# Layer 1's blocks of gated rows: their sums made in the up projection and loaded by the down projection

## The chip, the core and the metric

The kernel runs on one core of one Trainium2 chip. A core has four compute engines with a queue of instructions each: TensorE (PE, matrix products into PSUM), VectorE (DVE), ScalarE (ACT) and GpSimd (POOL). SyncE (SP) only issues transfers between the chip's memory (DRAM) and SBUF. The metric is the device time of one execution in microseconds, of which the median of several runs is taken. Profiled times of instructions are counted from the first instruction of the program.

## The reference, cut to what matters

Two layers of a diffusion backbone over 1024 tokens of width 1024. Each layer has a mixer (attention) and then a gated MLP with a width-3 convolution. The change is in the MLP of the last layer (layer 1), which has no context rows:

```python
def conv_ffn(x, w_up, conv_w, conv_b, w_down):
    h = x @ w_up                                   # 1024 x 1024 @ 1024 x 5632
    h = lax.conv_general_dilated(h, ...) + conv_b  # along the tokens, width 3
    a, g = jnp.split(h, 2, axis=-1)
    return (jax.nn.silu(g) * a) @ w_down           # 1024 x 2816 @ 2816 x 1024
```

All is float32. Each operand of a product is split into a rounded high part and the rest (`hi`, `lo`), and a product of two such operands takes three matmuls.

## The kernel before, in words

**Both products of the MLP go by a seven-product scheme** (Strassen's, in Winograd's form): each operand is cut in a 2 by 2 grid of blocks, seven products are made of blocks or sums of blocks in the place of eight, and their results are added up. The sums of blocks of `w_down` are made ahead of the layer and stored (`tD`); those of `w_up` are made by POOL when a tile is prepared (`sums`, tile `sw`). Those of the gated rows, which this change is about, are made in the down projection.

**The up projection** (`ffn_up`) goes over 22 tiles j (`NH = 22`), each 128 columns of `a` with the 128 columns of `g` that gate them. `one(j)` makes two of the seven products, `two(j)` the other five. Each product is 12 matmuls of 128x512 (L500 to L502). DVE adds them up in `z` (L479, L572), ACT and DVE make the convolution (L517; L518 and L519, two of each in a tile), ACT the SiLU (L578), DVE the product `silu(g) * a` (L579), and the tile (128 rows of the hidden matrix by 1024 tokens) is stored in DRAM as `hidD[j]` (L580). For layer 1 the first six tiles have their `one` ahead of all `two`s (`pre` is 6), then `one(j)`, `two(j)` follow each other. In this kernel the tiles come in the order 0, 1, 2, ... 21.

**The down projection** (`ffn_down`) sees the hidden matrix as blocks `a11` (tokens 0 to 511, tiles 0 to 10), `a21` (tokens 512 to 1023, the same tiles), `a12` and `a22` (tiles 11 to 21). The contraction goes in three chunks of 3, 4 and 4 tiles k (`CUT`), and in each chunk through the seven products in the order 1, 2, 5, 6, 7, 3, 4; such a pair of chunk and product is called an item here. An item is made for four pairs of token tiles p, so it has 4 times 3 n matmuls with n tiles in the chunk (L875 to L877, into `by` or `bj`). While the products of one item run, `prep` makes the operands of the next: `summed` forms the sum of blocks, in place (on POOL, L686):

```python
5: ("a21", "t1", ("a21", "a22", 1)),   6: ("a21", "t2", ("a21", "a11", 0)),
7: ("a11", "t3", ("a22", "a21", 0)),   3: ("a12", "b22", ("a12", "a21", 0)),
```

(the block that is overwritten, the weight block, and the two terms with 1 for plus), then `hidden` splits it in hi and lo: the rounding on ACT (L121), the rest on DVE (L122, a subtraction of two tiles in SBUF). `weight` does the same for the weight block (tiles `xm`, split into `whi` or `wlo`). In the trace the blocks `a11`, `a12` are called `xb` and `a21`, `a22` are called `a`. `collect` adds the product up in `y` (DVE or POOL, L738; the first copies on ACT, L785); in the last chunk ACT makes the squares for the norm (L337), and `finish` norms, adds the residual (L833) and stores the rows. Blocks are loaded from `hidD` by SP (L668), weight blocks from `w_down` or `tD` (L653).

**What sets the order**: every engine and SP work their queues in order. The order in the queues is made ahead of time by a planner, which follows the program's order and its own estimate of when each instruction could run, so that an instruction without a wait may stand earlier than the program has it. Tiles of a pool with one buffer (`bufs` 1) can be overwritten only when what read them is done. The tiles of the down projection's pool `dn` lie where the up projection's pool `up` was.

Of the kernel before, what the change touches and what calls it, by code (L numbers as in the profile page):

```python
# [12 lines left out]
ALU = mybir.AluOpType  # L13
# [4 lines left out]
P = 128  # L18
T = 1024
# [8 lines left out]
NH = DFF // P  # L28
HF = 512
# [26 lines left out]
class Net:  # L56
# [415 lines left out]

        return [first, lambda: sums(1), lambda: sums(2), lambda: part(load(NH + j) if ctx else load(NH + j)[:, HF:])]

    def ffn_up(self, l, ctx, pre, zb, pool, side=None):

        nc = self.nc
        V, G = nc.vector, nc.gpsimd
        add = lambda o, x, y, e=V: e.tensor_tensor(o, x, y, op=ALU.add)  # L479
        order = [(0, 0), (0, 3)] if ctx else [(0, 0)]  # L480
        order += [(j, 0) for j in range(1, pre)]
        order += [(j, i) for j in range(NH) for i in range(4) if (j, i) not in order]
        steps = [self.up_weights(l, j, ctx, pool, 2 <= j < pre) for j in range(NH)]
        ready, state = {}, {}
        X, Xc = {}, []

        def ahead(n):
            while order and len(ready) < n:
                j, i = order.pop(0)
                ready[j, i] = steps[j][i]()  # L490

        def take(j, i):
            ahead(4)
            return ready.pop((j, i))

        def product(W, v):
            hi, lo = X[v]
            o = self.t(self.by, [P, HF], "by")
            for k in range(4):
                nc.tensor.matmul(o, W[0][:, k, :], hi[k], start=(k == 0), stop=False)  # L500
                nc.tensor.matmul(o, W[0][:, k, :], lo[k], start=False, stop=False)  # L501
                nc.tensor.matmul(o, W[1][:, k, :], hi[k], start=False, stop=(k == 3))  # L502
            return o

        def plain(Ws):
            o = self.t(self.by, [P, HF], "by")[:, :C]
            for k in range(KD):
                W, (hi, lo) = Ws[k // 4], Xc[k]
                nc.tensor.matmul(o, W[0][:, k % 4, :], hi, start=(k == 0), stop=False)  # L509
                nc.tensor.matmul(o, W[0][:, k % 4, :], lo, start=False, stop=False)  # L510
                nc.tensor.matmul(o, W[1][:, k % 4, :], hi, start=False, stop=(k == KD - 1))  # L511
            return o

        def conv(o, z, nt):
            n = z.shape[1]
            cw = lambda i: self.cw[:, l, i, nt:nt + 1]
            nc.scalar.activation(o, z, AF.Identity, scale=cw(1), bias=cw(3))  # L517
            V.scalar_tensor_tensor(o[:, 1:], z[:, :n - 1], cw(0), o[:, 1:], op0=ALU.mult, op1=ALU.add)  # L518
            V.scalar_tensor_tensor(o[:, :n - 1], z[:, 1:], cw(2), o[:, :n - 1], op0=ALU.mult, op1=ALU.add)  # L519

        zt = lambda: self.t(pool(), [P, 1024], "z", zb)
        ot = lambda: self.t(pool(), [P, S if ctx else T], "o", 2)

        def one(j):

            a = take(j, 0)
            p1 = product(a[0], "B11")
            za = zt()
            nc.scalar.copy(za[:, HF:], p1)  # L529
            p2 = product(a[1], "B21")  # L530
            add(za[:, :HF], p2, za[:, HF:])
            oa = og = d = None
            rest = lambda: None
            if ctx:
                def rest():
                    conv(oa[:, T:], plain(a), j)
                if j == 0 or j >= pre:
                    oa = ot()
                    rest()
                if j == 0:  # L540
                    d = take(j, 3)
                    og = ot()
                    conv(og[:, T:], plain(d), NH + j)
            state[j] = za, oa, og, a, d

        def two(j, hook=None):
            za, oa, og, a, d = state.pop(j)
            C11, C12 = za[:, :HF], za[:, HF:]
            S1, S2 = take(j, 1)
            p6 = product(S2, "T2")  # L550
            add(C12, p6, C12)
            S3, S4 = take(j, 2)
            p7 = product(S3, "T3")
            if hook:
                hook()
            zg = zt()
            C21, C22 = zg[:, :HF], zg[:, HF:]
            add(C21, p7, C12)

            p5 = product(S1, "T1")  # L560
            add(C12, p5, C12)
            add(C22, p5, C21)
            p3 = product(S4, "B22")
            add(C12, p3, C12)
            if oa is None:
                oa = ot()
                if ctx:
                    conv(oa[:, T:], plain(a), j)
            conv(oa[:, :T], za, j)
            d = d or take(j, 3)  # L570
            p4 = product(d[0] if not ctx else d[1], "T4")
            V.tensor_tensor(C21, C21, p4, op=ALU.subtract)  # L572
            if og is None:
                og = ot()
                if ctx:
                    conv(og[:, T:], plain(d), NH + j)
            conv(og[:, :T], zg, NH + j)
            nc.scalar.activation(og, og, AF.Silu)  # L578
            self.last_gate = V.tensor_tensor(oa, oa, og, op=ALU.mult)  # L579
            (nc.scalar if j == NH - 1 and not ctx else nc.sync).dma_start(self.hidD[j], oa[:, :T])  # L580
            if ctx:
                c = max(i for i, x in enumerate(self.CUT[:-1]) if x <= j % (NH // 2))
                nc.sync.dma_start(self.hidC[c][j // (NH // 2)][:, :, j % (NH // 2) - self.CUT[c], :], oa[:, T:].rearrange("p (x n) -> p x n", x=2))

        def run(X_, Xc_, hook1, hook2):
            X.update(X_)
            Xc.extend(Xc_ or [])
            for j in range(pre):
                one(j)
            for j in range(NH):  # L590
                if j >= pre:
                    one(j)
                if side:
                    self.steps(side, 1 if j % 4 else 2)
                if j == NH - 1:
                    hook1()
                two(j, hook2 if j == NH - 1 else None)

        return lambda: ahead(2), run

# [28 lines left out]
            self.tc.keep_in_program_order(nc.sync.dma_start(self.tD[l][k], r))  # L629
            yield  # L630

    def ffn_down(self, l, ctx, A, blocks, units):


        nc = self.nc
# [3 lines left out]
        chunks = [range(x, y) for x, y in zip(self.CUT, self.CUT[1:])]  # L639
        res = {}  # L640
        cnt = [0, 0, 0]

        def load_b(c, nm, pin):
            f = int(nm[1]) - 1
# [13 lines left out]
        def weights(n):  # L658

            if n < len(items):  # L660
                load_b(items[n][0], self.FORM[items[n][1]][1], 4 <= n < 7)

        def load_a(c, nm):
            r, h = int(nm[1]) - 1, int(nm[2]) - 1
            res[nm] = []
            for i, k in enumerate(chunks[c]):
                x = blocks(nm, i)
                nc.sync.dma_start(x, self.hidD[k + h * (NH // 2)][:, r * HF:(r + 1) * HF])  # L668
                res[nm].append(x)
            if ctx:  # L670
                n = len(chunks[c])
                x = blocks(nm, 4)[:, :n * P]
                nc.sync.dma_start(x.rearrange("p (k n) -> p k n", k=n), self.hidC[c][h][:, r])
                res[nm].append(x)

        def prep(c, nm):

            a, b, asum = self.FORM[nm]
            n = len(chunks[c])
            nu = n + (1 if ctx else 0)  # L680
            o = ops[c, nm] = [None] * nu, [None] * n

            def summed(name, s, i, e):
                if s:
                    x, y, plus = s
                    e.tensor_tensor(res[name][i], res[x][i], res[y][i], op=ALU.add if plus else ALU.subtract)  # L686

# [49 lines left out]
        def run(src, dst, sink):  # L737
# [101 lines left out]
            for n, (c, nm) in enumerate(items):  # L839
# [4 lines left out]
                for p in range(np_):  # L844
                    if p == 4:
                        for f in early + late:
                            f()
                        early = late = []
                    cnt[2] += 1
                    o = self.t(*((self.by, [P, HF], "by") if cnt[2] % 6 < 4 else (self.bj, [P, HF], "bj")))  # L850
                    multiply(o, c, nm, p, 0, len(chunks[c]))
                    collect(c, nm, p, o)
# [26 lines left out]
    def mlp(self, xa, opA, l, ctx, yT, w_out, src, mid, dst, ahead=None, after=None):  # L879


        nc, tc = self.nc, self.tc
# [2 lines left out]
        A = lambda: self.t(xa, [P, HF], "xm", 16, F32R)  # L885
        mod = self.mod_cols(l, 1)
        halves = lambda x: x.rearrange("p (x n) -> p x n", x=2)
        with ExitStack() as e0:
            pool = lambda name, e: e.enter_context(tc.tile_pool(name=f"{name}{l}", reuse_waits="tile", bufs=1))
            xb = pool("xb", e0)  # L890

# [6 lines left out]
            with self.banks(out=4, turn=2):  # L898
              with self.banks(junk=1, tmp=1):
                with ExitStack() as e1:  # L900
                  xb2 = pool("xd", e1)
                  E = lambda dt=F32: self.t(xb2, [P, HF], "xd", 16, dt)
                  with ExitStack() as e2:
# [28 lines left out]
                      if l == 0:  # L932
                          side = self.ada_queue(lambda: up[0], [(1, b) for b in range(3)], bufs=1, small=lambda tag, p, n: self.t(up[0], [P, 2048], "awr", 1)[:p, :n] if tag == "adar" else self.t(up[0], [p, n], tag, 1),
                                                acc=lambda: self.t(self.bj, [P, HF], "bj"), turn=lambda: self.t(self.bt, [P, 512], "b1"))
                      start, run = self.ffn_up(l, ctx, 2 if ctx else 6, 3 if ctx else 7, lambda: up[0], side)

                      def rows(n):
                          res = []
# [42 lines left out]
                      where = list(range(28, 32)) + list(range(8)) + list(range(12, 16))  # L981
                  blocks = lambda nm, i: B(at[nm] + i).bitcast(F32) if nm in at else self.t(self.pp, [P, HF], f"{nm}_{i}", 1)
                  units = Units(lambda i: B(where[i]), len(where) // 2)
                  load_w, load_h, down = self.ffn_down(l, ctx, A, blocks, units)
                  with ExitStack() as e3:
                      up.append(pool("up", e3))

# [920 lines left out]
```

## Time and profile before

| | us |
|---|---|
| median of 3 runs (lowest, highest) | 2901.68 (2897.69, 2901.73) |
| the profiled execution | 2902.14 |
| its span, first to last instruction | 2900.3 |
| up projection of layer 1 in the trace | about 2243 to 2668 |
| down projection of layer 1 | about 2668 to 2901; last matmul ends at 2885 |

How to read the lines shown below: times are microseconds from the start of the span, means of single instructions are ns. "x11" is a count. `out<-in` are the tiles that an instruction writes and reads, by the program's names without numbers. In square brackets or behind a bar stands the idle time of the engine just ahead of the instruction, with what ended it. PEclk is the share of its clock that TensorE was granted. A row of stretches gives the busy time of each engine within it, so 20 of 20 is an engine without idle time. The ends of matmuls are modelled, and their busy times overlap.

### The profile page before, as it was taken

To read this page: it belongs to the slowest core of one execution; us is meant where nothing else is said; L and a number is where in the kernel's file an instruction comes from. 1 tells how busy PE (TensorE), PEld (TensorE's weight loads), DVE (VectorE), ACT (ScalarE), POOL (GpSimd) and SP (SyncE) were. 2 spreads that over 40 slices of the span, in tenths; PEclk is the share of its full clock that TensorE was granted. 3 is DMA by queue.
4 is the path that set the end of the run, shared out by engine and by line. 5 is a ranking of instruction groups with operands and counts; after the bars stand their busy time and mean duration, and the time that the engine had idled before them with its cause. 6 is when DMAs were issued, how large, how long until landed. Compare 5 with 4: busy or idle time off the path is not lost.

```text
span 2900.3 us, 42828 instructions
## 1 busy us (share of the span) xinstructions
PE 2795.5 (96%) x15699; PEld 2252.0 (78%) x15699; DVE 2125.2 (73%) x2645; ACT 1330.5 (46%) x2373; POOL 1497.5 (52%) x1396
## 2 busy tenths in 40 slices
PE   8999999999999999999989999999998999999997
PEld 6878977776888888878768986666677878887775
DVE  4451255569776777798988768888856898888999
ACT  4321066575333333444457545555556444444443
POOL 2231277446222222165767768888864543332766
PEclk9999999999999999999999999999999999999998
DMA  8366773554223333464244562232253222224642
GB/s 314 127 209 211 242 270 133 197 188 151 79 96 124 118 102 109 167 204 129 75 138 155 148 180 93 101 102 99 84 204 138 73 95 88 88 80 168 202 142 87
DMA packets 235650, 413.89 MB, mean 143 GB/s; under 512 B 28320, under 2 KB 133792, under 8 KB 227504
## 3 DMA queue, kind: packets, MB, share of 16 engines
q1 hardware_dynamic: 212736, 395.61, 40.5%
q10 hardware_dynamic: 22704, 15.55, 1.8%
q8 instruction: 124, 2.03, 0.3%
q14 instruction: 86, 0.70, 0.1%
HBM read 306.16 MB, written 104.92 MB: 142 GB/s over the span
## 4 chain that ended last, share of the span: by engine, by line
PE 55%; DVE 11%; POOL 6%; issue 4%; ACT 2%; DMA 2%; SPq 0%; DVEq 0%; POOLq 0%; ACTq 0%
PE by L500 8%; PE by L501 8%; PE by L502 8%; PE b L1703 4%; PE by L1715 4%; PE b L1684 3%; PE by L877 2%; PE by L875 2%; PE by L876 2%; DVE xb L122 2%; DVE wlo L122 2%; PE by L509 1%; PE by L511 1%; PE by L510 1%; POOL rstd L139 1%
## 5 line engine op out<-in xcount | busy, mean ns | idle before, releaser
L1727 POOL TENSOR_TENSOR part<-part,pT 128x512 f32<-128x512 f32 x192 | 271.6, 1415 | 14.4 <-ACT pT L1704 1.0
L463 POOL TENSOR_TENSOR sw<-wraw,wraw 128x512 f32<-128x512 f32 x44 | 61.0, 1386 | 422.2 <-DVE wlo L122 422.2
L122 DVE TENSOR_TENSOR wlo<-wraw,whi 128x1024 fp32r<-128x1024 f32 (+1 forms) x162 | 221.1, 1371 | 77.4 <-ACT whi L121 77.3
L479 DVE TENSOR_TENSOR z<-by,z 128x512 f32<-128x512 f32 x264 | 176.7, 684 | 106.5 <-PE by L502 103.7
L1704 ACT ACTIVATE pT<-b 128x512 f32<-128x512 f32 x320 | 170.4, 604 | 151.2 <-PE b L1703 137.4
L1685 DVE TENSOR_REDUCE ng<-b 128x1 f32<-128x1280 f32 x122 | 181.7, 1490 | 75.7 <-PE b L1684 75.3
L121 ACT CAST whi<-wraw 128x1024 fp32r<-128x1024 f32 (+1 forms) x162 | 159.5, 990 | 160.8 <-PE b L310 107.0
L500 PE MATMUL by<-xb,whi 128*128 128x512 f32 x528 | 208.0, 394 | 1.7 <-ACT xb L121 1.7
L502 PE MATMUL by<-xb,wlo 128*128 128x512 f32 x528 | 205.9, 390 | 1.0 <-DVE wlo L122 1.0
L501 PE MATMUL by<-xb,whi 128*128 128x512 f32 x528 | 206.2, 391 | 0.3 <-DVE xb L122 0.3
L121 ACT CAST xb<-xb 128x512 fp32r<-128x512 f32 (+2 forms) x184 | 103.2, 567 | 195.2 <-PE by L876 61.6
L615 POOL TENSOR_TENSOR ts<-ts 128x512 f32<-128x512 f32 x88 | 118.3, 1352 | 134.9 <-DMA ts<-in_w_down_dram 133.2
L121 ACT CAST whi<-sw 128x1024 fp32r<-128x1024 f32 x88 | 92.5, 1052 | 202.6 <-PE by L501 173.6
L518 DVE SCALAR_TENSOR_TENSOR o<-z,cw,o 128x1023 f32<-128x1023 f32 x88 | 141.2, 1605 | 48.7 <-ACT o L517 48.6
L122 DVE TENSOR_TENSOR xb<-xb,xb 128x512 fp32r<-128x512 f32 (+2 forms) x184 | 158.9, 879 | 19.4 <-ACT xb L121 18.2
L517 ACT ACTIVATE o<-z,cw 128x1024 f32<-128x1024 f32 x88 | 109.6, 1245 | 130.5 <-DVE z L479 109.0
L460 POOL TENSOR_TENSOR sw<-wraw 128x512 f32<-128x512 f32 x44 | 80.6, 1832 | 167.6 <-DVE wlo L122 124.7
L738 POOL TENSOR_TENSOR y<-y,wraw 128x512 f32<-128x512 f32 x72 | 116.2, 1636 | 94.0 <-DVE wraw L738 59.3
L1715 PE MATMUL by<-pT,Vs 128*64 128x256 f32 x1280 | 150.7, 382 | 0.0
L500 PE MATMUL by<-xm,whi 128*128 128x512 f32 x352 | 138.5, 393 | 4.6 <-ACT z L529 3.2
L500 PE MATMUL by<-xd,whi 128*128 128x512 f32 x352 | 137.4, 390 | 0.4 <-DVE z L479 0.3
L501 PE MATMUL by<-xm,whi 128*128 128x512 f32 x352 | 137.5, 391 | 0.0
(314 smaller groups left out, 8922.0 us busy)
## 6 DMA issues: line engine op xcount, KB each, us to landing
wraw<-in_w_up_t_dram SPq DMA_DIRECT2D x92, 512.0 KB
awr<-in_w_ada_dram SPq DMA_DIRECT2D x44, 1024.0 KB
ts<-in_w_down_dram SPq DMA_DIRECT2D x44, 512.0 KB
tD<-ts SPq DMA_DIRECT2D x22, 1024.0 KB
xm<-tD SPq DMA_DIRECT2D x88, 256.0 KB
hid<-o SPq DMA_DIRECT2D x43, 512.0 KB
xm<-in_w_down_dram SPq DMA_DIRECT2D x66, 256.0 KB
xb<-hid SPq DMA_DIRECT2D x66, 256.0 KB
```

Of the source, the lines that this page charges most:

```text
L121: x = nc.scalar.copy(hi, src) if hi_eng == "s" else nc.vector.tensor_copy(hi, src)
L122: y = (nc.gpsimd if lo_eng == "p" else nc.vector).tensor_tensor(lo, src, hi.bitcast(F32), op=ALU.subtract)
L479: add = lambda o, x, y, e=V: e.tensor_tensor(o, x, y, op=ALU.add)
L500: nc.tensor.matmul(o, W[0][:, k, :], hi[k], start=(k == 0), stop=False)
L501: nc.tensor.matmul(o, W[0][:, k, :], lo[k], start=False, stop=False)
L502: nc.tensor.matmul(o, W[1][:, k, :], hi[k], start=False, stop=(k == 3))
L518: V.scalar_tensor_tensor(o[:, 1:], z[:, :n - 1], cw(0), o[:, 1:], op0=ALU.mult, op1=ALU.add)
L615: sub = lambda o, x, y: nc.gpsimd.tensor_tensor(o, x, y, op=ALU.subtract)
L1685: nc.vector.tensor_reduce(b["ng"][:, h:h + 1], ps[:, :S], axis=AX.X, op=ALU.max, negate=True)
L1704: nc.scalar.activation(b["pT"][:, k], ps, AF.Exp)
L1715: nc.tensor.matmul(out(b["po"][:, :256], i), self.KV[b["g"]][2][:, k], two(b["pT"][:, k], i), start=(k == 0), stop=(k == NT - 1))
L1727: nc.gpsimd.tensor_tensor(x, x if k > 1 else b["pT"][:, 0], b["pT"][:, k], op=ALU.add)
```

## The change

For layer 1 alone, POOL makes the four sums of blocks during the up projection. A generator `hidden_sums` works pair by pair (tile k with tile k + 11): it loads the two tiles of 512 KB from `hidD`, makes the four sums in place in a buffer `hs` (one buffer), and stores the pair of 1 MB in a new DRAM tensor `sD`. So that pairs are complete early, the up projection takes its tiles in the order 0, 11, 1, 12, ... 10, 21. The generator takes its three steps per pair from the fourth tile on: one step after each tile, one more ahead of the `two` of each tile with an even number; what is left (the last two pairs) is done in the first items of the down projection, one step in every second product. In the down projection, `load_a` loads the sum for product 5 from `sD` in the place of `a21`, and `summed` is a load from `sD` of the next sum (256 KB, into the same tile that POOL overwrote before). Layer 0 is left as it was.

```diff
-    def ffn_up(self, l, ctx, pre, zb, pool, side=None):
+    def hidden_sums(self, l, pool):
         nc = self.nc
+        e = lambda o, x, y, op=ALU.subtract: nc.gpsimd.tensor_tensor(o, x, y, op=op)
+        for k in range(NH // 2):
+            r = self.t(pool, [P, 2, T], "hs", 1)
+            for h in range(2):
+                nc.sync.dma_start(r[:, h], self.hidD[k + h * (NH // 2)])
+            yield
+            (x, y), (u, v) = ((r[:, h, :HF], r[:, h, HF:]) for h in range(2))
+            e(v, v, y, ALU.add)
+            e(y, x, y)
+            yield
+            e(x, v, x)
+            e(u, u, x)
+            nc.sync.dma_start(self.sD[l][k], r)
+            yield
+
+    SUM = {5: (1, 1), 7: (0, 1), 6: (0, 0), 3: (1, 0)}
+
+    def ffn_up(self, l, ctx, pre, zb, pool, side=None, hs=None):
+        nc = self.nc
+        seq = [k + h * (NH // 2) for k in range(NH // 2) for h in range(2)] if hs else list(range(NH))
...
-        order += [(j, 0) for j in range(1, pre)]
-        order += [(j, i) for j in range(NH) for i in range(4) if (j, i) not in order]
-        steps = [self.up_weights(l, j, ctx, pool, 2 <= j < pre) for j in range(NH)]
+        order += [(j, 0) for j in seq[1:pre]]
+        order += [(j, i) for j in seq for i in range(4) if (j, i) not in order]
+        steps = {j: self.up_weights(l, j, ctx, pool, 2 <= n < pre) for n, j in enumerate(seq)}
...
-            for j in range(pre):
+            for j in seq[:pre]:
                 one(j)
-            for j in range(NH):
-                if j >= pre:
+            for n, j in enumerate(seq):
+                if n >= pre:
                     one(j)
...
-                two(j, hook2 if j == NH - 1 else None)
+                late = hs and n > 2
+                if late and n % 2 == 0:
+                    next(hs)
+                two(j, hook2 if n == NH - 1 else None)
+                if late:
+                    next(hs)
...
+        def made(x, k, nm):
+            h, r = self.SUM[nm]
+            nc.sync.dma_start(x, sD[k][:, h, r * HF:(r + 1) * HF])
+
         def load_a(c, nm):
...
-                nc.sync.dma_start(x, self.hidD[k + h * (NH // 2)][:, r * HF:(r + 1) * HF])
+                if sD and nm == "a21":
+                    made(x, k, 5)
+                else:
+                    nc.sync.dma_start(x, self.hidD[k + h * (NH // 2)][:, r * HF:(r + 1) * HF])
...
             def summed(name, s, i, e):
-                if s:
+                if s and sD and i < n:
+                    if nm != 5:
+                        made(res[name][i], chunks[c][i], nm)
+                elif s:
                     x, y, plus = s
                     e.tensor_tensor(res[name][i], res[x][i], res[y][i], op=ALU.add if plus else ALU.subtract)
...
                     cnt[2] += 1
+                    if hs and cnt[2] % 2:
+                        next(hs, None)
...
+        self.sD = {}
         with ExitStack() as e0:
+            hsum = None
+            if not ctx:
+                self.sD[l] = [self.t(self.dr, [P, 2, T], f"sD{l}_{k}") for k in range(NH // 2)]
+                hsum = self.hidden_sums(l, e0.enter_context(tc.tile_pool(name=f"hs{l}", reuse_waits="tile", bufs=1, side="right")))
```

More of the change, by code (lines that the diff above doesn't have):

```diff
@@ L536, in rest @@
                     conv(oa[:, T:], plain(a), j)
-                if j == 0 or j >= pre:
+                if j == 0 or j not in seq[:pre]:
                     oa = ot()
@@ L587, in run @@
             Xc.extend(Xc_ or [])
-            for j in range(pre):
+            for j in seq[:pre]:
                 one(j)
-            for j in range(NH):
-                if j >= pre:
+            for n, j in enumerate(seq):
+                if n >= pre:
                     one(j)
                 if side:
-                    self.steps(side, 1 if j % 4 else 2)
-                if j == NH - 1:
+                    self.steps(side, 1 if n % 4 else 2)
+                if n == NH - 1:
                     hook1()
-                two(j, hook2 if j == NH - 1 else None)
+                late = hs and n > 2
[4 more added lines that the diff above has]
+                    next(hs)
         return lambda: ahead(2), run
@@ L630, in down_sums, with ffn_down @@
             yield
-    def ffn_down(self, l, ctx, A, blocks, units):
+    def ffn_down(self, l, ctx, A, blocks, units, hs=None):
         nc = self.nc
@@ L641, in ffn_down @@
         cnt = [0, 0, 0]
+        sD = self.sD.get(l)
         def load_b(c, nm, pin):
@@ L934, in mlp @@
                                                 acc=lambda: self.t(self.bj, [P, HF], "bj"), turn=lambda: self.t(self.bt, [P, 512], "b1"))
-                      start, run = self.ffn_up(l, ctx, 2 if ctx else 6, 3 if ctx else 7, lambda: up[0], side)
+                      start, run = self.ffn_up(l, ctx, 2 if ctx else 6, 3 if ctx else 7, lambda: up[0], side, hsum)
                       def rows(n):
@@ L983, in mlp @@
                   units = Units(lambda i: B(where[i]), len(where) // 2)
-                  load_w, load_h, down = self.ffn_down(l, ctx, A, blocks, units)
+                  load_w, load_h, down = self.ffn_down(l, ctx, A, blocks, units, hsum)
                   with ExitStack() as e3:
```

## The prediction

> **What bounds the kernel now.** The page's first part first: which engine fills the span.
>
> ```profile
> PE 2795.5 (96%) x15699; PEld 2252.0 (78%) x15699; DVE 2125.2 (73%) x2645; ACT 1330.5 (46%) x2373; POOL 1497.5 (52%) x1396
> ```
>
> TensorE fills it; a change that removes no matmul can win only where PE waits. So next the busy times by stage, layer 1's MLP from the second halves of its first six tiles to the end.
>
> ```profile
> core 0: us, PE busy (x) PEld busy (x) DVE busy (x) ACT busy (x) POOL busy (x), PEclk, DMA share, GB/s
> 2283.00:2365.00 82.00, 80.54 (x349) 64.55 (x348) 78.45 (x76) 35.36 (x35) 35.58 (x21) 1.00 0.28 97
> 2365.00:2640.00 275.00, 275.00 (x1214) 227.22 (x1213) 234.69 (x236) 114.45 (x118) 91.81 (x58) 1.00 0.23 82
> ...
> 2668.00:2700.00 32.00, 26.17 (x105) 20.20 (x104) 29.34 (x31) 18.55 (x33) 15.24 (x9) 0.95 0.71 231
> 2700.00:2780.00 80.00, 80.00 (x354) 66.02 (x353) 80.00 (x91) 33.38 (x62) 53.90 (x34) 1.00 0.56 183
> 2780.00:2840.00 60.00, 57.78 (x247) 47.01 (x246) 56.40 (x59) 25.99 (x52) 50.51 (x30) 0.97 0.31 95
> 2840.00:2886.00 46.00, 41.79 (x174) 33.19 (x172) 44.20 (x56) 15.09 (x35) 28.79 (x27) 0.96 0.14 51
> ```
>
> The up projection holds PE at 275 of 275 us with 40.3 us of DVE idle. In the down projection (2668 to 2886, 218 us) PE is idle 5.83 + 0 + 2.22 + 4.21 = 12.3 us, and DVE is busy 29.34 + 80 + 56.4 + 44.2 = 209.9 us, 96%. What PE waits for there:
>
> ```profile
> PE by L875 <- ACT y L785: 3.5, 1, 3.5
> PE by L877 <- DVE xb L122: 2.7, 3, 1.6
> PE by L876 <- DVE whi L122: 1.9, 2, 1.1
> PE bj L876 <- DVE whi L122: 1.9, 1, 1.9
> PE by L876 <- DVE wlo L122: 1.3, 1, 1.3
> ```
>
> All but the first are waits for DVE's splits (the columns are us in all, times, longest). The timeline shows a price beyond the wait, here after the longest one, which ends at 2672:
>
> ```profile
> 2674.07 0.63 PE L877 MATMUL by<-whi,xb 128*128 128x512 f32 x1
> 2674.50 0.63 PE L875 MATMUL by<-wlo,xb 128*128 128x512 f32 x1
> ```
>
> These start 0.43 us apart; undisturbed it is 275 / 1214 = 0.23. Some eight to ten matmuls run at that pace after the waits at 2672 and 2792 (the one of 1.9 into `bj`), 0.2 us each: 2 us more. So the four places cost about 5.5 us (2672), 3 (2690 to 2696, the waits for `xb`), 4 (2792) and 5 (2870 to 2875: the last three waits' 3.2 and a slow stretch, PEclk 0.96).
>
> Why DVE is full: the groups of splits in the down projection (2675 to the end; count, busy us, mean ns of one), two splits side by side, and two of the four groups of sums that go.
>
> ```profile
> L738 POOL TENSOR_TENSOR y<-y,wraw 128x512 f32<-128x512 f32 x32 | 53.0, 1680 | 41.6 <-DVE wraw L738 25.4 <-ACT wraw L785 16.2
> L122 DVE TENSOR_TENSOR xb<-a,xb 128x512 fp32r<-128x512 f32 x33 | 44.7, 1358 | 3.6 <-ACT xb L121 3.6
> L122 DVE TENSOR_TENSOR wlo<-xm,wlo 128x512 fp32r<-128x512 f32 x33 | 42.1, 1277 | 0.9 <-ACT wlo L121 0.9
> ...
> L122 DVE TENSOR_TENSOR xb<-xb,xb 128x512 fp32r<-128x512 f32 x38 | 37.0, 979 | 0.0
> L122 DVE TENSOR_TENSOR whi<-xm,whi 128x512 fp32r<-128x512 f32 x33 | 35.3, 1070 | 0.0
> ```
> ```profile
> 2773.94 1.77 DVE L122 TENSOR_TENSOR xb<-xb,xb 128x512 fp32r<-128x512 f32 x1
> 2775.63 0.68 DVE L122 TENSOR_TENSOR wlo<-xm,wlo 128x512 fp32r<-128x512 f32 x1
> ```
> ```profile
> L686 POOL TENSOR_TENSOR a<-a,a x11: 1272/1733/2271, 2661.8 to 2796.0; 128x512 f32<-128x512 f32 x11
> L686 POOL TENSOR_TENSOR a<-a,xb x11: 1667/1735/1748, 2679.8 to 2827.1; 128x512 f32<-128x512 f32 x11
> ```
>
> A split takes 0.68 us or 1.77, and POOL's sums stretch from 1.27 to 1.73: the two stand in each other's way. Over 0.68 us the four groups lose 33 x 0.68 + 33 x 0.60 + 38 x 0.30 + 33 x 0.39 = 66 us. POOL runs 85 operations of this shape there: 41 of L686, 40 adds of L738 (32 in the row), 4 of the gate. So one costs DVE 0.78 us.
>
> The Trainium skill, "SBUF — State Buffer", section "Who interferes with whom", says that a DVE instruction with two SBUF inputs and a GpSimd instruction that reads SBUF take the same port as an exclusive lock, and that the later one waits until the first is done. This trace agrees where the two meet (1.77 is 0.68 and most of POOL's 1.27).
>
> **The change, part by part.**
>
> *Removed: 44 sums on POOL in the down projection* (four groups of x11; three sums run from 2661.8). Eight of the moved ones, for pairs 9 and 10, may still run after 2640. So 36 to 40 sums fewer, times 0.78: DVE loses 28 to 31 us of its 210. What each waiting place gets of it:
>
> - 2672. Three sums block the convolution of the last tile, whose end lets the first copy into `y` start:
>
> ```profile
> 2661.76 6.10 POOL L686 TENSOR_TENSOR a<-a,a 128x512 f32<-128x512 f32 x3 [24.48 <-DMA a<-hid]
> ```
> ```profile
> 2660.37 1.28 DVE o L518
> 2662.17 2.32 DVE o L519
> 2664.49 2.24 DVE o L518
> 2666.75 2.21 DVE o L519
> ```
>
> (the latter from the chain of waits). Three of the four passes take 2.2 to 2.3 us where 1.28 would do: 2.9 us of the 3.5 waited. Without them the wait nearly goes and the slow stretch with it: -5 at best; 0 if pair 9's sums slip into the same gap of POOL. I take -3.5.
> - 2690 to 2696: -3 at best, since all DVE splits there are blocked; but see the transfers below. I take -2.
> - 2792: the wait itself lies under eight of POOL's adds, which stay (next fence), but DVE comes to it without one idle moment from 2700 to 2780, behind by chunk 1's sixteen sums. I take -3.5 of 4.
> - 2870: the same run of eight adds. They start late since DVE took up the products late, again after a stretch full of sums (2780 to 2840, where POOL is busy for 50.51 of 60 us). I take -2; bounds -5 and 0.
>
> ```profile
> 2778.20 13.18 POOL L738 TENSOR_TENSOR y<-y,wraw 128x512 f32<-128x512 f32 x8 [3.04 <-DVE wraw L738]
> 2858.75 12.74 POOL L738 TENSOR_TENSOR y<-y,wraw 128x512 f32<-128x512 f32 x8 [3.04 <-DVE wraw L738]
> ```
>
> What is late next there is that run of adds itself.
>
> *Added: 44 sums in the up projection* (36 certainly).
>
> ```profile
> L518 DVE SCALAR_TENSOR_TENSOR o<-z,cw,o 128x1023 f32<-128x1023 f32 x29 | 53.9, 1860 | 20.9 <-ACT o L517 20.9
> L519 DVE SCALAR_TENSOR_TENSOR o<-z,cw,o 128x1023 f32<-128x1023 f32 x30 | 44.3, 1477 | 0.0
> ```
>
> From 2365 to 2640 POOL's 58 operations cost the convolution 29 x 0.58 + 30 x 0.20 = 23 us over 1.28 each, 0.4 us an operation. These are 15 tiles (30 passes of L519), 18.3 us each, so some 30 sums more: 12 to 23 us (0.4 to 0.78 each) against 40.3 us of DVE idle: covered. The first pair's four sums may fall before 2365, where DVE has 3.55 us idle in 82 and PE already lost 1.46: 4 x 0.4 to 4 x 1.1 us. POOL's own weight sums wait behind a pair of sums for up to 3.5 us; POOL is idle two thirds of the time (91.81 of 275). I take +1; bounds 0 and +5.
>
> *Added transfers.* In the up projection 2.1 MB per pair, in 37 us: 57 GB/s on top of 82, at a DMA share of 0.23. Hidden. SP waits for the sums before it stores a pair, and the weight loads queue behind; the planner can put the store where the sums are done. Nothing, +2 at worst. In the down projection product 5's loads replace others, and 33 loads of 256 KB are new (8.4 MB). SP can issue product 6's load only when product 5's split has read the tile, as POOL's sum had to wait, but 1.7 us of POOL become a transfer:
>
> ```profile
> 2680.43 4.91 DMA xm<-in_w_down_dram
> ...
> 2785.17 2.73 DMA xm<-tD
> ```
> ```profile
> q1 hardware_dynamic: 6085, 12.15, 88.5%
> ```
>
> 2.7 us in a quiet stretch, 4.9 in the busy one (the last row is 2674 to 2714: 12.15 MB in 40 us are 304 GB/s, and the queue is 88.5% full). An item lasts 36 or 48 matmuls of 0.23, 8 or 11 us, and its operands are made one item ahead, so 1 to 3 us more is covered, except early, where 2.3 MB of chunk 0's sums and up to 3 MB of pairs 9 and 10 join. I take +1.5; bounds 0 and +8.
>
> *Order of tiles, SBUF, the 15 us after the last stretch above*: nothing; no wait of them rests on a sum of blocks or on which tile comes first.
>
> Sum: -3.5 - 2 - 3.5 - 2 + 1 + 1.5 = -8.5, so 2902.1 (the profiled execution; 1.8 us lie around its span) becomes 2893.6. It stands 0.5 us over the median of the runs, which I leave: **2893.5**.
>
> **Rivals.**
>
> 1. *The relief doesn't reach PE* (about 2900). POOL's adds hold both late waits, pair 9's sums take the gap at 2661, the start drowns in transfers: only -3.5 is left, less 2.5. For it: the two x8 rows. Against: DVE is full only because of the sums.
> 2. *Each moved sum blocks DVE as long as at its worst*, 1.1 us (1.77 - 0.68): a pair's four fall in one tile, 4.4 us against 40.3 / 15 = 2.7 idle. That is 1.7 over in each of eight pairs, 14 in all; where half of it isn't made up in the next tile, PE loses 7 and the gain is nearly gone: 2900 to 2902. For it: the conv rows at 2.3. Against: 0.4 us an operation in the same stage now, since DVE idles or reads PSUM for part of the time. The Trainium skill's "SBUF — State Buffer" (the section named above), read strictly, gives this case.
> 3. *The start of the down projection starves* (slower). Between 2674 and 2714 there are 40 us with 4.6 us of free transfer time. If 5.3 MB more must pass there at 304 GB/s, that is 17 us, 13 beyond what is free. The loads for product 6 queue behind them; once the queue grows over the 8 us of an item, PE waits: +13 with slow stretches, -5 elsewhere: 2910. For it: the chain of waits already passes through the 4.91 us load at 2680. Against: of the 17, pair 9's 2 MB can go earlier, and most loads are for items far ahead.
> 4. *All waits for splits and the copy go*: -5 - 3 - 4 - 5 = -17, 2885.
>
> **How the numbers follow.** Forecast (-6 to -14) 0.40, rival 4 0.13, rival 1 0.20, rival 2 0.12, rival 3 0.15. A measurement of this kernel tells about 0.2%, 5.8 us, from no change. Forecast and rival 4 are faster (a little of the forecast's upper end counts as same), 1 and 2 the same, 3 nearly all slower: faster 0.52, same 0.34, slower 0.14. The range goes from rival 4's 2885 to 2906, which leaves out most of rival 3; the forecast alone has 2888 to 2897.
>
> **What would show it.** Right: no sums L686 on POOL after 2700 and splits near 0.8 us in place of 1.0 to 1.36; DVE's busy share of the down projection near 83%; last tile's convolution at 1.3 us a pass, PE's wait at 2672 under 1 us. The up projection still 275 of 275 for PE. Wrong: PE waits in the up projection on `z` or `wlo`; ACT's rounding of the blocks waiting for a load from `sD`; SP standing at a store of a pair; or POOL's sums of pairs 9 and 10 inside 2660 to 2690.

## The result and the profile after

The change makes the kernel slower: 2923.65 us (median of 4 runs, 2922.45 to 2927.54) against 2899.68 beside it (2894.61 to 2901.73), a ratio of 1.0088, 95% interval [1.0070, 1.0105]. The prediction was 2893.5, with a range from 2885 to 2906. The profiled execution after took 2923.73 us; its span is 2921.9. First part of the page after:

```profile
PE 2799.9 (96%) x15699; PEld 2250.6 (77%) x15699; DVE 2105.4 (72%) x2645; ACT 1326.7 (45%) x2373; POOL 1504.4 (51%) x1396
```

The same matmuls in a longer span: PE waits more. Where, is seen from the matmuls of the two products, before and then after (the two numbers behind the durations are the first and the last start; the first line is of the up projection, the second of the down projection):

```profile
L500 PE MATMUL by<-xm,whi x176: 389/389/794, 2218.4 to 2642.2; 128*128 128x512 f32 x176
...
L877 PE MATMUL by<-whi,xb x104: 387/389/628, 2657.0 to 2884.6; 128*128 128x512 f32 x104
```
```profile
L525 PE MATMUL by<-xm,whi x176: 389/389/794, 2216.6 to 2667.6; 128*128 128x512 f32 x176
...
L922 PE MATMUL by<-whi,xb x104: 388/389/498, 2684.1 to 2905.6; 128*128 128x512 f32 x104
```

From the first matmul of up to the first of down (the first is at 2218.4, earlier than the "about 2243" of the table of before): 2657.0 - 2218.4 = 438.6 us before, 2684.1 - 2216.6 = 467.5 after, so **+28.9**. From there to the last start in down: 227.6 before, 221.5 after, so **-6.1**. Up began 1.8 earlier in this execution and the end of the program took 0.6 longer, which makes the 21.6 between the spans (2900.3, 2921.9). The down projection gained, and the up projection, costed at +1, lost more than four times that gain.

The stretches of after (columns as in the prediction's table of stretches):

```profile
2283.00:2365.00 82.00, 76.91 (x330) 60.76 (x330) 77.10 (x73) 34.08 (x35) 47.32 (x27) 1.00 0.42 144
2365.00:2640.00 275.00, 259.70 (x1120) 208.26 (x1118) 233.86 (x212) 99.53 (x107) 141.16 (x82) 1.00 0.36 130
...
2700.00:2730.00 30.00, 23.31 (x92) 18.69 (x91) 17.09 (x25) 12.67 (x23) 7.02 (x5) 0.89 0.94 338
2730.00:2860.00 130.00, 130.00 (x575) 107.67 (x574) 106.68 (x147) 57.77 (x111) 46.78 (x31) 1.00 0.64 212
2860.00:2907.00 47.00, 46.00 (x203) 37.74 (x202) 42.49 (x57) 19.22 (x42) 25.75 (x25) 1.00 0.14 49
```

PE, 275 of 275 before, has 259.7 of 275 in the up projection, with no engine full in its place: DVE has 41 us idle. That is a chain of waits, not a full engine. In the down projection PE stands once for long, between 2700 and 2730, and then runs nearly to the end without a gap.

**The up projection after: a load at the head of POOL's queue.** The waits of POOL from 2365 to 2640 (us in all, times, longest; "issue" means that the profile names nothing that ended the wait):

```profile
POOL sw L463 <- DVE wlo L122: 44.0, 7, 7.9
POOL hs L479 <- DMA hs<-hid: 41.2, 4, 10.4
...
POOL hs L479 <- issue: 21.1, 3, 10.3
```

In six of the seven pairs there the first of the four sums (L479) keeps POOL standing for 10 us. The chain of waits shows for what, and what comes behind it:

```profile
2493.44 1.14 DVE o L604
...
2494.60 2.78 DMA hid<-o
...
2497.40 3.46 DMA hs<-hid
...
2501.02 1.30 POOL hs L479
2502.32 2.23 POOL sw L463
2504.55 1.26 POOL sw L464
...
2505.83 1.05 ACT whi L121
```

DVE ends a tile (L604), the tile is stored (2.78 us), and the same tile is loaded again for its sums (3.46). The planner has put the first sum ahead of POOL's two later weight sums of the next tile (L463, L464), which have nothing to do with the gated rows; they wait with it, then ACT's rounding of `sw`, then DVE's split, then PE. POOL's timeline shows the rest of the pair (in square brackets the idle time before):

```profile
2501.02 1.30 POOL L479 TENSOR_TENSOR hs<-hs 128x512 f32<-128x512 f32 x1 [10.39 <-DMA hs<-hid]
2502.27 2.28 POOL L463 TENSOR_TENSOR sw<-wraw,wraw 128x512 f32<-128x512 f32 x1
2504.51 1.29 POOL L464 TENSOR_TENSOR sw<-wraw,sw 128x512 f32<-128x512 f32 x1
2505.76 5.23 POOL L479 TENSOR_TENSOR hs<-hs 128x512 f32<-128x512 f32 x3
2510.95 2.27 POOL L460 TENSOR_TENSOR sw<-wraw 128x512 f32<-128x512 f32 x1
```

Three more sums hold the next tile's first weight sum (L460) for 5.2 us. ACT's, DVE's and PE's waits in the same projection, after (PE's from 2283 to 2640):

```profile
ACT whi L121 <- POOL sw L464: 41.1, 13, 6.2
...
DVE wlo L122 <- ACT whi L121: 21.0, 6, 3.5
...
PE by L525 <- DVE z L504: 8.5, 9, 1.7
PE by L527 <- DVE wlo L122: 7.2, 10, 1.5
PE by L525 <- ACT whi L121: 4.6, 6, 0.9
```

Before, the first of these was 6.1 us over 14 times and the second wasn't there: DVE itself now stands for 3.5 us, six times. The ends of DVE's products `silu(g) * a` (one in a tile) give the pace: 19.0 and 19.0 us in a pair of tiles before, 17.7 and 23.5 after, 41.2 in place of 38.1. The first pairs lose more than this 3.1, since before they ran at DVE's 17.7 a tile, catching up.

**The down projection after.** Its one long wait, in the chain of waits:

```profile
2697.95 7.23 DMA hid<-o
...
2705.20 0.32 SPq L685
...
2705.56 3.59 DMA xm<-tD
...
2710.50 7.00 DMA a<-sD
...
2717.52 0.63 ACT xb L121
2718.15 0.04 issue
2718.19 0.79 PE by L920
2718.99 0.43 PE by L921
```

SP, which works its queue in order, stands at a weight load (L685) until the last tile is stored, 6.2 us. The loads of blocks from `sD` are behind it in the queue; the chain reaches them through the weight load that stood (3.59 us) and two of DVE's splits (2709.55 to 2710.50). Then one takes 7.00 us, in a stretch with a DMA share of 0.94. PE's longest wait there:

```profile
PE by L920 <- ACT xb L121: 6.7, 1, 6.7
```

Before, SP stood at that place too (14.6 us, for the same store), but product 6's operands were sums of blocks that lay in SBUF, and POOL needed no queue of transfers for them.

### The profile page after: what moved, and what is told of

Read it like the earlier page. It is cut to its first block, busy times and chain, and to the rows that moved or that the text cites. A ratio compares the mean times of both kernels' runs of the same rounds, so it can differ in the third digit from the quotient of the medians.

```text
span 2921.9 us, 42936 instructions
## 1 busy us (share of the span) xinstructions
PE 2799.9 (96%) x15699; PEld 2250.6 (77%) x15699; DVE 2105.4 (72%) x2645; ACT 1326.7 (45%) x2373; POOL 1504.4 (51%) x1396
## 5 line engine op out<-in xcount | busy, mean ns | idle before, releaser
L122 DVE TENSOR_TENSOR wlo<-wraw,whi 128x1024 fp32r<-128x1024 f32 (+1 forms) x162 | 233.8, 1449 | 79.8 <-ACT whi L121 79.0
L463 POOL TENSOR_TENSOR sw<-wraw,wraw 128x512 f32<-128x512 f32 x44 | 68.0, 1545 | 338.9 <-DVE wlo L122 338.9
L122 DVE TENSOR_TENSOR xb<-xb,xb 128x512 fp32r<-128x512 f32 (+2 forms) x184 | 152.6, 844 | 17.9 <-ACT xb L121 15.4
L460 POOL TENSOR_TENSOR sw<-wraw 128x512 f32<-128x512 f32 x44 | 86.3, 1961 | 134.8 <-DVE wlo L122 99.4
```

Of the source, the lines that this page charges most:

```text
L122: y = (nc.gpsimd if lo_eng == "p" else nc.vector).tensor_tensor(lo, src, hi.bitcast(F32), op=ALU.subtract)
```

## The experiments

Paces and stages were read as above from each profile: us in a pair of tiles in the middle of the up projection; up from its first matmul to its last; down from there to the last matmul. "before" is the median of the runs of the kernel before on the same chip.

| kernel | median | before | ratio [95%] | pair | up | down |
|---|---|---|---|---|---|---|
| before | 2899.68 | | | 38.1 | 438.3 | 228.3 |
| after | 2923.65 | 2899.68 | 1.0088 [1.0070, 1.0105] | 41.2 | 467.2 | 222.2 |
| e1_older_pair | 2923.13 | 2898.52 | 1.0077 [1.0051, 1.0102] | 41.2 | 474.6 | 214.3 |
| e2_no_sums | 2888.76 | 2898.52 | 0.9957 [0.9941, 0.9974] | 38.1 | 439.9 | 215.8 |
| e3_down_loads_only | 2887.79 | 2898.52 | 0.9964 [0.9946, 0.9981] | 38.1 | 438.2 | 215.3 |
| e4_behind_weight_sums | 2900.42 | 2898.52 | 1.0002 [0.9986, 1.0018] | 38.6 | 446.6 | 221.3 |
| e5_bunch | 2902.47 | 2902.14 | 1.0004 [0.9987, 1.0020] | 36.9 to 38.1 | 447.5 | 218.5 |
| e6_one_sum | 2903.30 | 2902.14 | 1.0010 [0.9996, 1.0024] | 39.1 | 448.6 | 219.2 |
| e7_half | 2897.79 | 2902.14 | 0.9981 [0.9968, 0.9994] | 37.6 | 441.3 | 217.4 |
| e8_three_per_tile | 2917.22 | 2902.14 | 1.0053 [1.0034, 1.0071] | 38.4 | 453.4 | 228.2 |
| e9_split_old_pair | 2910.95 | 2898.60 | 1.0047 [1.0032, 1.0061] | 39.1 | 452.5 | 225.1 |
| e10_half_bunch | 2893.07 | 2898.60 | 0.9981 [0.9973, 0.9990] | 37.0 to 38.1 | 442.4 | 217.5 |

The theory put forward first, A in the expectations: the sum that waits for the fresh tile, ahead of the weight sums, is what costs. Its rivals: the transfers; the sums as work that blocks DVE; and the sums' place, several of them between POOL's weight sums whether they wait or not (D; in e9's expectation, B).

**Take the wait away, first try (e1).** The sums take tiles of two pairs earlier.

```diff
-                nc.sync.dma_start(r[:, h], self.hidD[k + h * (NH // 2)])
+                nc.sync.dma_start(r[:, h], self.hidD[max(k - 2, 0) + h * (NH // 2)])
```

> The changed kernel, but the buffer of pair k is loaded with the tiles of pair k-2 (0 for the first two), which lie in memory long since; as many transfers, sums and stores. The sums are of other tiles than the reference wants. Theory A (POOL stands in its queue for the load of a tile stored just before, 10 us in each pair, and the weight sums behind it come late): POOL's waits for hs loads go, PE's waits in the up projection drop from 22 us to under 8, total 2895 to 2905. Theory B (the 44 sums themselves, by blocking DVE): PE's waits stay above 15 us, total above 2912. Theory C (the extra transfers): as B.

The time did not move, but neither did the wait. The planner, free to issue earlier, put the loads two pairs earlier, from the sixth pair on again right behind the store of the tile they read. POOL's waits in e1:

```profile
POOL hs L479 <- DMA hs<-hid: 58.3, 7, 10.3
```

So this one tells nothing between the theories; it tells that an older operand alone doesn't give a later place.

**Leave out the sums (e2), and the loads and stores of the up projection as well (e3).** In e2 the four `e(...)` of `hidden_sums` go and its loads and its store stay. In e3 nothing of `hidden_sums` is left, and the down projection loads blocks of `hidD` of the same size in the place of the sums.

> The changed kernel without the four POOL sums of each pair: the pair is loaded and stored as it is, so the down projection gets blocks in the place of their sums. Theories A and B: the up projection is back at 19.0 us a tile, total 2885 to 2897 (the gain of the down projection alone, less its wait of 6.9 us at the start if that stays). Theory C: the up projection stays at 20.6 us a tile, total above 2910.

> Only the down projection's part: no pairs are summed or stored, the tiles come in the order 0, 1, 2, ..., and the loads that would fetch a sum fetch a plain block of the hidden matrix (so what is multiplied isn't the sum). This is what the relief of POOL and DVE in the down projection is worth by itself. By the prediction's terms -8 to -17, 2883 to 2893. If the wait for product 6's operands at the start (6.9 us after the change) comes of the 256 KB loads alone it stays: 2892 to 2897; if it comes of the transfers of the last pairs it goes: 2880 to 2888.

The two are alike, and both faster than before. e2's up projection, at a DMA share of 0.39, against 0.23 before:

```profile
2365.00:2640.00 275.00, 275.00 (x1214) 227.19 (x1213) 232.33 (x237) 113.44 (x117) 96.06 (x59) 1.00 0.39 139
```

PE is busy throughout, as before, and up is 1.6 us longer (439.9 against 438.3). The transfers are not what costs, so the rest of this is about the sums. The relief of the down projection is real: e3's is 13.0 us shorter than before (228.3 to 215.3), by the ratio some 10 us of the run (2898.5 x 0.0036, between 5.5 and 15.7), and PE waits there but once:

```profile
PE by L920 <- ACT xb L121: 3.9, 1, 3.9
```

**Put the sums behind the weight sums (e4).** Two sums in every tile, behind L461, at a point where their pair has landed (`sw1` is the instruction of L461).

```diff
-            e(v, v, y, ALU.add)
-            e(y, x, y)
+            with self.tc.issue_after(self.sw1.ins):
+                e(v, v, y, ALU.add)
+                e(y, x, y)
             yield
-            e(x, v, x)
-            e(u, u, x)
+            with self.tc.issue_after(self.sw1.ins):
+                e(x, v, x)
+                e(u, u, x)
             nc.sync.dma_start(self.sD[l][k], r)
-            yield
...
                 late = hs and n > 2
-                if late and n % 2 == 0:
-                    next(hs)
```

> The changed kernel with all its work, but two sums at a time stand in POOL's queue behind the second weight sum of a tile (L461), and the load of a pair stands a tile later, behind a store that is long done. Theory A: no wait of POOL for hs loads, PE's waits in the up projection under 6 us, total 2890 to 2900. Theory B: the sums block DVE as before, PE loses 2 us or more in each pair, total above 2910.

Most of the loss is gone, 1.0002 in place of 1.0088, with every sum still made in the up projection. What is left is DVE, in e4's stretch and in DVE's waits there:

```profile
2365.00:2640.00 275.00, 273.85 (x1192) 221.26 (x1191) 253.44 (x228) 106.75 (x114) 154.70 (x87) 1.00 0.36 132
...
DVE o L543 <- ACT o L542: 19.5, 14, 1.7
```

DVE is idle for 21.6 us, and 19.5 of them are a wait of 1.4 us in every tile for ACT's first pass of the convolution, which has no other work of DVE to fill it. So DVE has nothing left, and each tile takes 19.3 us. The same view of before:

```profile
DVE o L518 <- ACT o L517: 20.9, 15, 1.7
DVE z L479 <- PE by L502: 18.4, 22, 1.5
```

Only the second row is time that DVE could give, and nearly all of it lies behind 2440. In the four tiles that end from 2387 to 2440 DVE catches up and sets the pace, with no wait for PE, at 17.7 us a tile; against PE's 19.0 that leaves 1.3 of cover a tile. Two sums take more: (19.3 - 17.7) / 2 = 0.8 us a sum.

**Four sums in one bunch (e5).** As e4, but all four in every second tile, behind L461.

```diff
             with self.tc.issue_after(self.sw1.ins):
                 e(v, v, y, ALU.add)
                 e(y, x, y)
-            yield
-            with self.tc.issue_after(self.sw1.ins):
                 e(x, v, x)
                 e(u, u, x)
```

> As the kernel with the sums behind the weight sums (e4), but all four sums of a pair stand in one bunch, in every second tile, with no load to wait for. Theory A (POOL standing for a fresh load ahead of the weight sums makes most of the loss): two tiles stay near 38.6 us as in e4, total 2898 to 2904. Theory D (the bunch itself, four sums side by side, makes it): two tiles near 41 us as in the changed kernel, total above 2912.

POOL then holds its later weight sums for 8 us at a stretch,

```profile
2530.46 8.12 POOL L479 TENSOR_TENSOR hs<-hs 128x512 f32<-128x512 f32 x4
2539.74 1.30 POOL L463 TENSOR_TENSOR sw<-wraw,wraw 128x512 f32<-128x512 f32 x1 [1.16 <-DVE wlo L122]
```

and the pace isn't hurt: 17.2 and 19.7 us, 36.9 in a pair while DVE catches up, and PE's 38.1 later. From 2400 to 2640 PE has no wait at all. Up is 9.2 us longer than before all the same: PE's waits from 2283 on, 8.5 us in all (before: 1.3), lie ahead of 2400, with the first pairs' sums, where DVE has little to give (before, it is busy for 78.45 of the 82 us from 2283 to 2365). A bunch without a load to wait for, in that place, is harmless once DVE has caught up.

**One sum, with the wait (e6).** After, with only the first of the four sums.

```diff
             e(v, v, y, ALU.add)
-            e(y, x, y)
             yield
-            e(x, v, x)
-            e(u, u, x)
```

> The changed kernel with only the first of the four sums of each pair (the other three are left out, so what the down projection loads isn't all sums); this one still stands ahead of a weight sum in POOL's queue and waits for the load of the tile stored just before. Theory A: the late tile of a pair loses some 3 us, two tiles take 39.5 to 41 us, total 2900 to 2912. Theory D: one sum costs DVE 0.8 us and is covered, two tiles take 38.1 us, total 2886 to 2893.

The wait is there (`hs` waited for 51.2 and 10.8 us in seven pairs), and a pair takes 39.1: 1.0 above PE's 38.1. DVE's wait for ACT's rounding is there as in after, 21.1 us in six waits. A single waiting sum costs something, but less than half of after's 3.1. The wait alone, as a fixed price, doesn't explain after.

**The same order without the wait (e9).** To take the two apart: POOL's queue as in after, one sum ahead of L463 and three behind L464 in every second tile, but of a pair whose last tile was stored nearly two tiles earlier; in the middle of up its load is issued at 2506.7 and its first sum starts at 2523.4. Against e5 (`sw2` is the instruction of L464):

```diff
             with self.tc.issue_after(self.sw1.ins):
                 e(v, v, y, ALU.add)
+            with self.tc.issue_after(self.sw2.ins):
                 e(y, x, y)
                 e(x, v, x)
                 e(u, u, x)
```

> The kernel after the change with its own order on POOL (one sum of blocks of gated rows directly ahead of the two later weight sums of a tile, the other three right behind them, in every second tile), but the four sums take a pair that was loaded about two tiles earlier. The place of the sums is the same, the load to wait for is gone; in five-microsecond terms: POOL's first sum, which stood 10.4 us behind the landing of the fresh tile, should start as soon as the weight sum ahead of it is done. Theory A (the wait for the fresh load is what costs): a pair of tiles falls from 41.2 us back to 38 to 38.6, the up projection from 467 us to 445 to 450, the run 2895 to 2906. Theory B (the place of the sums between and behind the weight sums costs by itself, whether they wait or not): a pair stays at 40.5 to 41.2, up at 460 to 470, the run 2915 to 2925. Half way (39.2 to 40, 2906 to 2914) would say that both are needed: three late sums behind the weight sums and the wait ahead of them.

Half way, as the expectation's last case has it (the pair at 39.1 just below its 39.2). POOL and DVE in e9:

```profile
POOL sw L463 <- DVE wlo L122: 92.9, 14, 7.2
...
DVE o L543 <- ACT o L542: 19.5, 14, 1.7
```

No sum waits for a load any more; POOL waits for DVE, and DVE, with nothing but its 1.4 us a tile idle, sets 39.1 us a pair. With the wait it is 41.2.

DVE's pace adds this up. Without sums its own round is 35.4 us a pair (2 x 17.7), 2.7 under PE's 38.1: that is all the cover there is. The wait (3.5 of DVE's time in each pair) and one sum make 39.1 in e6; four sums without a wait make 39.1 in e9. Each is 3.7 over the round and so 1.0 over PE. In after both are there, 5.8 over the round, and the cover is there but once: 3.1 over PE.

So the up projection's 28.9 us come apart, in steps from one profile to the next: transfers and the order of tiles 1.6 (438.3 to 439.9, e2), four sums a pair behind L461 7.6, all with the first pairs (e5, 447.5), their place on both sides of L463 and L464 5.0 (e9, 452.5), the wait for the fresh tile 14.7 (467.2). Each step rests on one profile of each kernel. The runs' ratios rise in the same order, 0.9957, 1.0004, 1.0047, 1.0088, by some 12 to 14 us each time; in e9's share of that are 6.6 us of the down projection (225.1 against e5's 218.5), where PE waits for operands again:

```profile
PE by L918 <- ACT xb L121: 5.9, 3, 2.6
PE bj L920 <- DVE xb L122: 3.9, 1, 3.9
```

Why that start is worse in e9 than in e5 wasn't followed up.

**Three sums in a tile (e8).** As e4, with a third sum `e(v, v, y)` in each half, which spoils the stored sums; it was to test the 0.8 us a sum.

> e4 with a third sum per tile beside its two (it repeats a subtraction, so the sums are wrong). If DVE's chain is the bound from the second sum on, a tile takes 17.7 + 3 x 0.8 = 20.1 us in place of 19.3, and the total grows by 12 to 16 us over e4: 2911 to 2917. If PE still has cover, it stays within 4 us of e4.

It failed: a pair takes 38.4, less than e4's 38.6 with four sums. The loss came elsewhere, in the last two tiles (25.5 and 25.9 us) and in the down projection. POOL's first weight sum there waits for its load, not for DVE:

```profile
POOL sw L460 <- DMA wraw<-in_w_up_t_dram: 72.5, 13, 8.4
```

Another order of POOL's work against DVE's, so another price. 0.8 us is e4's price and no constant; why e8's is lower stays open.

**Versions that beat both: half of the sums (e7, e10).** Only the sums for products 5 and 7 are made in the up projection, behind L461; POOL makes those for 6 and 3 in the down projection as before. e7 has one of them in every tile, e10 both in every second one (the only difference):

```diff
             with self.tc.issue_after(self.sw1.ins):
                 e(v, v, y, ALU.add)
-            yield
-            with self.tc.issue_after(self.sw1.ins):
                 e(y, x, y)
             nc.sync.dma_start(self.sD[l][k], r[:, :, HF:])
+            yield
```

> A version that gives the reference's result: two of the four sums (products 5 and 7) are made in the up projection, one per tile, behind the weight sums; the down projection loads those and makes the other two on POOL as before. If a sum costs DVE 0.8 us and DVE's own work of a tile takes 17.7 us against 19.0 of PE, one per tile is covered: 19.0 us a tile; the down projection gains most of what it gains without sums. Total 2888 to 2895, faster than both. If DVE's idle time were no cover, 2898 or more.

> Only the sums for products 5 and 7 are made in the up projection, both in one bunch in every second tile behind the first two weight sums; products 6 and 3 keep their sums on POOL in the down projection, as before the change. A candidate for the best version, beside the earlier run that had one such sum in every tile (2897.8 us, up 441.3 us, down 217.4 us). If a bunch is cheaper for DVE than the same sums spread over the tiles, as the bunch of four (37 to 38 us a pair) against two a tile (38.6) suggests: up 439 to 441, run 2888 to 2895. If spreading makes no difference: 2895 to 2900, like the earlier run.

Both are 0.9981 of before, with intervals below 1, and the same within them, so spreading made no difference that these runs show. e7's tiles took 18.8 us, so a single sum in a tile cost DVE 1.1 (18.8 - 17.7) and was covered; its time missed the forecast of 2888 to 2895. In e10's down projection (217.5 us) no wait of PE is longer than 1.3:

```profile
PE by L915 <- DVE wlo L122: 1.3, 1, 1.3
```

The stall of after's start isn't there, though SP stands for the last store all the same, 9.8 us: product 6's operand comes from POOL. e3's 2887.8, which makes no sums, shows how far it could go.

## Why the prediction was wrong

**Relief of the down projection: right, and a little too small.** The prediction's four terms make -11 (-3.5, -2, -3.5, -2); e3 measures -13.0 in the profile, with a stall of 3.9 still in it. The late waits at 2792 and 2870 went altogether, rival 4's case. The last tile's convolution took 1.2 to 1.3 us a pass, as foretold; PE's wait behind it shrank from 3.5 to 1.7, not below 1. DVE is busy for 181.67 of the 223 us from 2684 to 2907, 81%, where 83 was said. The slowest and the fastest group of splits after 2700:

```profile
L122 DVE TENSOR_TENSOR wlo<-xm,wlo 128x512 fp32r<-128x512 f32 x33 | 31.3, 948 | 0.0
...
L122 DVE TENSOR_TENSOR whi<-xm,whi 128x512 fp32r<-128x512 f32 x34 | 26.8, 789 | 2.8 <-ACT whi L121 2.6
```

From 0.79 to 0.95 us in the mean, near the 0.8 that was named.

**Transfers in the down projection: inside the bounds, above the value.** The term was +1.5 (0 to +8). After's down projection is 6.9 us longer than e3's (222.2 against 215.3). Rival 3 had the right place and a price too high (13): the loads for product 6 did come late, but once, and behind SP's wait for a store as much as behind bytes. e3, without the pairs' transfers, still waits 3.9 us there, and e2, with them, 4.6. That e7 and e10, without that load, don't stall points the same way; no run moved the load in SP's queue alone.

**Sums in the up projection: the step that failed, +28.9 for +1 (0 to +5).** Two sentences of it were wrong.

- *"12 to 23 us (0.4 to 0.78 each) against 40.3 us of DVE idle: covered."* The price was in reach (0.8 in e4), the cover wasn't: 20.9 of the 40.3 us were DVE's own wait for ACT in each tile. With 18.4 us of real cover against 24 (30 x 0.8), the same sum would have said that DVE becomes the bound. The prediction's own row of L518 has the 20.9 (`<-ACT o L517`); the sum didn't take it off. Rival 2 was this case at 1.1 us a sum; four sums cost DVE 1.5 us a pair in e5 (36.9 less 2 x 17.7), 3.2 in e4 and 3.7 in e9. Ahead of 2365 the prediction allowed 1.6 to 4.4 us for one pair; two pairs' sums ran there (2316 to 2357), and PE lost 3.6 us more than before (5.1 of the 82 against 1.5), so that part fits its bounds. The Trainium skill, "SBUF — State Buffer", section "Who interferes with whom", says that the order of issue decides which of the two engines is held up. Prices that change with the place in POOL's queue agree with it; the order at the port itself is seen in no run here.
- *"POOL's own weight sums wait behind a pair of sums for up to 3.5 us; POOL is idle two thirds of the time."* It asked how long the sums run and not when their operand lands. The wait that POOL brought to its own queue was 10.4 us, and a share of idle time is no answer to a wait at the head of a queue in order. Its sign was listed ("PE waits in the up projection on `z` or `wlo`"), its cause was not among the rivals.

SP at the store of a pair, which the prediction looked at, was harmless: the store (L492) goes at 2511.01, when the three sums end at 2510.99. It looked at the transfer behind the sums and not at the one ahead of them.

## What to carry to other kernels

Work that is moved under another stage brings its wait to every queue that it enters: ask when its operand lands, and what stands behind it in that queue, before asking whether the engine has idle time. Of an engine's idle time only that which waits for the bounding engine is cover; what it waits for in its own chain in each round is not. And where a planner sets the order, an operand that is ready earlier is used earlier, so a wait is removed by fixing the place, not by older data.

## What the runs showed of the hardware

A tile just stored and loaded back through DRAM took 2.78 + 3.46 = 6.2 us until POOL could use it, in a stretch with a DMA share of 0.36. A load of 256 KB took 7.00 us at a share of 0.94.

After's 6.7-us wait of PE is followed by matmuls 0.43 us apart (PEclk 0.89). The 19 gaps in its up projection between 2365 and 2640, 0.92 to 1.86 us from start to start in the trace, are not: the next start comes 0.34 later, and nearly all others there are 0.23 apart, at a PEclk of 1.00. Short gaps cost little beyond themselves here.
